# The first feed-forward stage grouped 4, 6, 6, 6 like the second, and low weight parts made by accumulating DMAs

## The chip, the cores and the metric

The kernel runs on one core of a Trainium2 chip. The metric is the device time in microseconds (us) of one execution; three runs of the kernel before took 881.19, 881.35 and 881.50 us, a median of 881.35. TensorE (PE) multiplies, VectorE (DVE), ScalarE (ACT) and GpSimd (POOL) work elementwise, SyncE (SP) issues most of the DMAs, and POOL can issue DMAs as well.

## The reference

One layer of an encoder on 512 positions of width 1024, in float32; the two feed-forward halves are what the change touches:

```python
def swiglu(h, w_gate, w_up, w_down):
    return (jax.nn.silu(h @ w_gate) * (h @ w_up)) @ w_down      # D_FF = 2752

x = x + 0.5 * swiglu(rms_norm(x, ffn1_norm), ffn1_w_gate, ffn1_w_up, ffn1_w_down)
h = rms_norm(x, mix_norm); u = h @ w_in          # Fourier mixer, attention
...
x = x + concat([f_out, a_out]) @ w_out
x = x + 0.5 * swiglu(rms_norm(x, ffn2_norm), ffn2_w_gate, ffn2_w_up, ffn2_w_down)
return rms_norm(x, final_norm)
```

## The kernel before

Every float32 operand is split in two parts: the high part is the value rounded to TensorE's fp32r format, the low part is the rest. A product of two such operands is three matmuls (`product`, L100 to L103): high by high, high by low, low by high. For a weight tile the high part is a cast on ACT (L96) and the low part a subtraction on VectorE (`lows`, L72): `lo = raw - hi`. The raw tile comes by a DMA on SP's queue (`raw_tile`, L85 to L88) into one of three buffers.

The hidden width of 2752 is cut into 21 columns of 128 and a tail "t" of 64. A feed-forward stage (`ffn`) goes through its columns in four groups; after each group the down products of its columns are added to `x`, one for each of the eight blocks `d` of the output (`down`, with weights `raw_dn`; `residual`, L390).

A column is computed in one of two ways. In the first group it is *plain*: a gate and an up product (`gate(c)`, c = 2j and 2j + 1), each of 8 x 3 = 24 matmuls with 512 columns; `evacuate` multiplies by the norm's row, applies the silu and splits the result into `at`. In later groups it is made of *seven products* of half the size (`seven`, L304): 7 x 4 x 3 = 84 matmuls with 256 columns, whose weight operands are sums of quarters (`prepare`), and whose moving operands `rt` are made once for a stage, in four steps, by `operands`, between the plain gates. Group g's seven-products are run ahead by one column: the first group holds its last plain column over to the second group (`rest`).

The weights' parts lie in slots of 4 KB for each partition: the ring has 12, of which 8 hold the normalised input (`hh`, `hl`) in the first group and become the pool of the seven-products later; the other 4 rotate (`plain`, `slot()`). In a first group four more are lent from free places of `at` (`lent`): two are handed back (`back(lent[:2])`) after the opening, two before the last gate.

The stage's opening makes the first gates: in stage 1 four together (`opening1`: columns 0 and 1), in stage 2 two, one behind the other (column 0). The tail's gate follows (`gate(2 * NF)`), then the other plain gates (`left`). In the last group of a stage the first two down products start without the group's last column, and that column's ending (`rest`) stands between them.

The orders on PE and SP are as written (`in_order`); those on ACT, VectorE and POOL are made by the framework's scheduler. The power of each norm, which the norm's row needs, runs on POOL (L160), and so do three loads ahead of the mixing stage (L842).

Of the kernel before, what the change touches and what calls it, by code (L numbers as in the profile page):

```python
# [9 lines left out]
AF = mybir.ActivationFunctionType  # L10
ALU = mybir.AluOpType
# [5 lines left out]
KD = D // P  # L17
F = 2752
NF = F // P
# [5 lines left out]
FILL_LEAD = 0.1  # L25
NS = 12

GROUPS1 = ((0, "t", 1, 2, 3), range(4, 10), range(10, 15), range(15, 21))
GROUPS2 = ((0, "t", 1, 2), range(3, 9), range(9, 15), range(15, 21))
PLACES = 7  # L30
HALF = S // 2
USES = "a11", "a12", "s1", "s2", "s4", "s3", "a22"
# [6 lines left out]
def asf(ap):  # L39
    return ap.bitcast(F32)  # L40
# [3 lines left out]
def encoder(ctx, tc, A, out):  # L44
    nc = tc.nc
# [36 lines left out]
    def weight_slots():  # L82
        return (slot().rearrange("p (a b) -> p a b", b=P) for _ in range(2))

    def raw_tile(src, name, n=KD):  # L85
        raw = wp.tile([P, KD, P], F32, tag="raw", name=f"raw_{name}")
        nc.sync.dma_start(out=raw[:, :n, :], in_=src)
        return raw  # L88

    def weights(src, name, n=KD, raw=None):  # L90
        raw = raw or raw_tile(src, name, n)
        hi, lo = weight_slots()
        if name in HI_DVE:
            nc.vector.tensor_copy(hi[:, :n, :], raw[:, :n, :])
        else:
            nc.scalar.copy(hi[:, :n, :], raw[:, :n, :])  # L96
        lows(lo[:, :n, :], raw[:, :n, :], hi[:, :n, :])
        return hi, lo
# [76 lines left out]
            nc.scalar.copy(self.rb[:, t], ps[:, t])  # L175
            return ps

    def ffn(norm, after, wgu, wd, wdt, groups, opening, closing):

        n_ = norm.n
        n_plain = len(groups[0])
        with tc.tile_pool(name=f"act{n_}", bufs=1) as ap, tc.tile_pool(name=f"sums{n_}", bufs=2) as sp:
            at = ap.tile([P, PLACES, 2, S], F32R, name=f"at{n_}")
            rt = ap.tile([P, 7, 2, KH, HALF], F32R, name=f"rt{n_}")
# [6 lines left out]

            own, shared = slots[:KD], slots[KD:]

            def gate(c, between={}):
                whi, wlo = weights(wgu[c], f"gu{n_}_{c}")
                ps = bank(f"gu{n_}_{c}")
                for k in range(KD):  # L200
                    between.get(k, int)()
                    product(ps, whi[:, k, :], wlo[:, k, :], hh[k], hl[k], k == 0, k == KD - 1)
                return ps
# [34 lines left out]
            def back(ts):  # L238
                plain[:] = [t for t in plain if all(t is not q for q in ts)]
# [12 lines left out]
            def prepare(j, most=False):  # L252

                g = sp.tile([P, KD * P], F32, tag="raw_g", name=f"raw_g{n_}_{j}")
                u = wp.tile([P, KD * P], F32, tag="raw", name=f"raw_u{n_}_{j}")
                for t, c in ((g, 2 * j), (u, 2 * j + 1)):
                    nc.sync.dma_start(out=t.rearrange("p (a b) -> p a b", b=P), in_=wgu[c])
                a11, a12, a21, a22 = g[:, :S], g[:, S:], u[:, :S], u[:, S:]
                s12 = sp.tile([P, 2 * S], F32, tag="s12", bufs=1, name=f"s12_{n_}_{j}")
                s34 = sp.tile([P, 2 * S], F32, tag="s34", bufs=1, name=f"s34_{n_}_{j}")  # L260
                w = {}

                def both(names, src):
                    hi, lo = (take(most and names[0] != "a11") for _ in range(2))
                    nc.scalar.copy(hi, src)  # L265
                    lows(lo, src, hi)
                    for i, n in enumerate(names):
                        w[n] = tuple(t[:, i * S : (i + 1) * S] for t in (hi, lo))
                    w[max(names, key=USES.index), "slots"] = hi, lo

                def single(n, src):
                    t = take(False)
                    hi, lo = t[:, :S], t[:, S:]
                    nc.scalar.copy(hi, src)
                    lows(lo, src, hi)
                    w[n] = hi, lo
                    w[n, "slots"] = (t,)

                def combine(out, a, b, op):
                    nc.vector.tensor_tensor(out=out, in0=a, in1=b, op=op)  # L280

                return w, [
                    (both, ("a11", "a12"), g),
                    (combine, s12[:, :S], a21, a22, ALU.add),
                    (combine, s12[:, S:], s12[:, :S], a11, ALU.subtract),
                    (both, ("s1", "s2"), s12),
                    (single, "a22", a22),
                    (combine, s34[:, :S], a11, a21, ALU.subtract),
                    (combine, s34[:, S:], a12, s12[:, S:], ALU.subtract),
                    (both, ("s3", "s4"), s34),  # L290
                ]
# [100 lines left out]
                )  # L392

            every = slice(0, S)
            for gi, group in enumerate(groups):
                last = gi == len(groups) - 1
                ahead = []
                if gi:
                    rest = seven(range(group[0] + 1, min(group[-1] + 2, NF)), ready)
                else:  # L400
                    lent = [at[:, i].rearrange("p a b -> p (a b)") for i in range(PLACES - 4, PLACES)]
                    plain.extend(lent)
                    row = []
                    pss = dict(enumerate(opening(gate, lambda: norm.column([norm.acc]), lambda: row.append(norm.row()))))
                    back(lent[:2])
                    due, parts, left = [*pss, "t"], list(range(KH)), range(2 * len(pss), 2 * n_plain)
                    pss["t"] = [gate(2 * NF)]
                    tail_weights()
                    for i, c in enumerate(left):
                        if c == left[-1]:  # L410
                            back(lent)
                        pss.setdefault(c // 2, []).append(gate(c))
                        if due:
                            j = due.pop(0)
                            evacuate(at[:, place(j)], n_, pss[j], norm)
                        if c % 2 and c != left[-1]:
                            due.append(c // 2)
                        while len(parts) * len(left) > (len(left) - 1 - i) * KH:
                            o = parts.pop(0)
                            operands(row[0], o, o + 1)  # L420

                    def rest():
                        evacuate(at[:, place(n_plain - 1)], n_, pss[n_plain - 1], norm)

                def added(d, ps):
                    residual(d, ps, every)
                    if last:
                        (after.sums if closing else after.add)(d)
                    if ahead:
                        f, *a = ahead.pop(0)  # L430
                        f(*a)

                waiting = []
                for d in range(KD):
                    if last and d == KD - 2:
                        back(lent)
                        if closing:
                            closing([(e, down(e, group, gi)) for e in (d, d + 1)], residual)
                            break
                    ps = bank(f"dn{n_}_{d}_{gi}")  # L440
                    steps = down(d, group, gi)(ps, every)
                    for _ in range(len(group) - (last and d < 2)):
                        next(steps)
                    waiting.append((d, ps, steps))
                    if d == 1 and not last:
                        ready = prepare(groups[gi + 1][0] + 1)
                        ahead.extend(ready[1])
                    if d == 0:
                        rest()
                        if last:  # L450

                            lent = slots[KD - 2 : KD]
                            plain[:0] = lent
                            continue
                    for d_, ps, steps in waiting:
                        for _ in steps:
                            pass
                        added(d_, ps)
                    waiting = []
                for f, *a in ahead:  # L460
                    f(*a)
                free.extend(where[j] for j in group)

    def evacuate(at, n_, pss, norm):
# [32 lines left out]
    n0, n1 = Norm(0), Norm(1)  # L497
# [42 lines left out]
        return [pss[0:2], pss[2:4]]  # L540

    with in_order():
        ffn(n0, n1, A["wgu1"], A["wd1"], A["wdt1"], GROUPS1, opening1, None)


    n2 = Norm(2)
    with tc.tile_pool(name="mix", bufs=1) as mp, tc.tile_pool(name="mixt", bufs=1) as mt:
# [281 lines left out]
        scale = HD**-0.5  # L829
# [95 lines left out]
    n3 = Norm(3)  # L925

    ready = (3, 4, 5)
# [50 lines left out]
        finish(2, 4)  # L978

    with in_order():  # L980
        ffn(n2, n3, A["wgu2"], A["wd2"], A["wdt2"], GROUPS2, lambda gate, column, row: [[gate(0, {KD - 1: column}), gate(1, {3: row})]], closing)


def _order():
# [101 lines left out]
```

## Time and profile before

| | |
|---|---|
| runs | 881.19, 881.35, 881.50 us |
| the profiled execution | 882.0 us, span 880.1 us, mean granted PE clock 0.995 |
| busy of the span | PE 863.1 us, VectorE 640.4, ACT 451.0, POOL 24.7 |
| stage 1, from the page's rows and the timeline | opening to 31.4 us, the tail's gate and six plain gates to 70.1, first group's down products to 96.0, seven-products and down products to 353.2 |
| mixing stage | 353 to about 524 us |
| stage 2 | about 524 us to the end |
| DMA | 83.37 MB on SP's queue, 1.32 MB on POOL's |

A PE matmul of 512 columns has a duration of 395 ns in the rows, but the next one starts about 0.23 us later; one of 256 columns has 283 ns and a step of 0.12. So the steps between starts are used for sums, not the durations. "idle <-" names what ended an engine's wait.

### The profile page before, as it was taken

How to read it: one execution, taken by the hardware profiler on the slowest of the kernel's cores; microseconds unless marked ns; L12 is line 12 of the kernel's file. 1: busy time of each engine (PE TensorE's matmuls, PEld its weight loads, DVE VectorE, ACT ScalarE, POOL GpSimd, SP SyncE). 2: the span in 40 equal slices, each digit the busy share in tenths (PEclk: the TensorE clock that was granted, in tenths of full speed). 3: DMA queues.
4: the chain of work that ended last, by engine and by line, in shares of the span. 5: the costliest groups of instructions: out<-in, count | busy, mean ns of one | idle time of the engine just before them, and what ended most of it. 6: DMA issues, size and time to landing. Idle time of an engine off the chain costs nothing.

```text
span 880.1 us, 13432 instructions
## 1 busy us (share of the span) xinstructions
PE 863.1 (98%) x5334; PEld 766.7 (87%) x5334; DVE 640.4 (73%) x1003; ACT 451.0 (51%) x746; POOL 24.7 (3%) x32
## 2 busy tenths in 40 slices
PE   8999999999999999999999999999999999999995
PEld 5888999889989988888888888889998999889985
DVE  7798788459757837699888558977975688469444
ACT  7454466226525634677775436535652365327432
POOL 0000000000000000211000000000000000000002
PEclk9999999999999999999999999999999999999998
DMA  7324232333243113521110223242224232322212
GB/s 245 112 67 164 98 118 86 99 116 104 69 141 114 55 36 108 204 83 37 50 48 25 94 67 127 75 141 97 108 79 140 88 119 69 105 110 85 73 36 96
DMA packets 29150, 85.55 MB, mean 97 GB/s; under 512 B 3488, under 2 KB 6560, under 8 KB 28960
## 3 DMA queue, kind: packets, MB, share of 16 engines
q1 hardware_dynamic: 28560, 83.37, 28.1%
q0 software_dynamic: 384, 1.32, 0.5%
q8 instruction: 41, 0.67, 0.3%
q14 instruction: 21, 0.17, 0.1%
q10 hardware_dynamic: 144, 0.02, 0.0%
HBM read 81.81 MB, written 2.10 MB: 95 GB/s over the span
## 4 chain that ended last, share of the span: by engine, by line
PE 56%; issue 39%; DVE 2%; ACT 2%; DMA 1%; POOL 0%; SPq 0%; POOLq 0%; ACTq 0%; DVEq 0%
PE r L304 10%; PE q L304 5%; PE dn L103 4%; PE dn L101 4%; PE dn L102 4%; PE p L304 3%; PE gu L103 2%; PE gu L102 2%; PE gu L101 2%; PE out L101 2%; PE out L103 2%; PE out L102 2%; PE pt L790 1%; PE q L101 1%; PE q L102 1%
## 5 line engine op out<-in xcount | busy, mean ns | idle before, releaser
L304 PE MATMUL r<-rt,ring 128*128 128x256 f32 x1584 | 207.2, 283 | 0.0
L304 PEld LDWEIGHTS r<-rt,ring 128*128 128x128 f32 x1584 | 196.1, 188 | 2.4
L101 PE MATMUL dn<-at,ring 128*128 128x512 f32 x324 | 128.0, 395 | 0.8 <-ACT ring L96 0.8
L103 PE MATMUL dn<-at,ring 128*128 128x512 f32 x324 | 127.9, 395 | 0.3 <-DVE ring L72 0.3
L102 PE MATMUL dn<-at,ring 128*128 128x512 f32 x324 | 127.9, 395 | 0.0
L390 DVE SCALAR_TENSOR_TENSOR xt<-dn,xt 128x512 f32<-128x512 f32 x62 | 42.8, 690 | 89.4 <-PE dn L103 89.4
L304 PE MATMUL q<-rt,ring 128*128 128x256 f32 x792 | 104.8, 282 | 0.0
L96 ACT CAST ring<-raw_dn 128x768 fp32r<-128x768 f32 (+3 forms) x64 | 48.1, 754 | 108.2 <-PE dn L102 89.8
L304 PEld LDWEIGHTS q<-rt,ring 128*128 128x128 f32 x792 | 98.7, 188 | 0.0
L72 DVE TENSOR_TENSOR ring<-s,ring 128x1024 fp32r<-128x1024 f32 x66 | 80.3, 1220 | 16.7 <-PE r L304 9.7
L265 ACT CAST ring<-s 128x1024 fp32r<-128x1024 f32 x66 | 69.3, 1050 | 37.4 <-PE r L304 19.2
L103 PEld LDWEIGHTS dn<-at,ring 128*128 128x128 f32 x324 | 61.0, 188 | 15.2 <-DVE ring L72 0.7
L101 PEld LDWEIGHTS dn<-at,ring 128*128 128x128 f32 x324 | 60.9, 188 | 14.8 <-ACT ring L96 1.0
L102 PEld LDWEIGHTS dn<-at,ring 128*128 128x128 f32 x324 | 60.9, 188 | 13.9
L72 DVE TENSOR_TENSOR ring<-raw_dn,ring 128x768 fp32r<-128x768 f32 (+3 forms) x64 | 54.5, 854 | 11.3 <-ACT ring L96 8.9
L304 PE MATMUL p<-rt,ring 128*128 128x256 f32 x396 | 52.4, 282 | 0.0
L72 DVE TENSOR_TENSOR ring<-raw_g,ring 128x1024 fp32r<-128x1024 f32 x33 | 40.4, 1223 | 15.5 <-PE p L304 10.9
L304 PEld LDWEIGHTS p<-rt,ring 128*128 128x128 f32 x396 | 49.3, 188 | 0.0
L265 ACT CAST ring<-raw_g 128x1024 fp32r<-128x1024 f32 x33 | 34.6, 1049 | 22.9 <-PE r L304 9.9
L101 PE MATMUL gu<-ring 128*128 128x512 f32 x112 | 44.1, 394 | 0.9 <-ACT ring L527 0.9
L102 PE MATMUL gu<-ring 128*128 128x512 f32 x112 | 43.9, 392 | 0.0
L103 PE MATMUL gu<-ring 128*128 128x512 f32 x104 | 41.1, 395 | 0.8 <-DVE ring L72 0.7
(308 smaller groups left out, 1514.0 us busy)
## 6 DMA issues: line engine op xcount, KB each, us to landing
raw_g<-in_wgu SPq DMA_DIRECT2D x33, 512.0 KB, 3.7
raw_u<-in_wgu SPq DMA_DIRECT2D x33, 512.0 KB, 4.3
raw_dn<-in_wd SPq DMA_DIRECT2D x40, 384.0 KB, 3.0
raw_gu<-in_wgu SPq DMA_DIRECT2D x16, 512.0 KB, 3.6
raw_o<-in_wo SPq DMA_DIRECT2D x8, 512.0 KB, 3.5
raw_in<-in_wins SPq DMA_DIRECT2D x6, 512.0 KB, 4.1
raw_dn<-in_wd SPq DMA_DIRECT2D x8, 320.0 KB, 2.9
raw_dn<-in_wd SPq DMA_DIRECT2D x8, 256.0 KB, 2.6
```

The source lines that it names most:

```text
L72: nc.vector.tensor_tensor(out=lo, in0=src, in1=asf(hi), op=ALU.subtract)
L96: nc.scalar.copy(hi[:, :n, :], raw[:, :n, :])
L101: nc.tensor.matmul(ps, whi, mhi, start=first, stop=False)
L102: nc.tensor.matmul(ps, whi, mlo, start=False, stop=False)
L103: nc.tensor.matmul(ps, wlo, mhi, start=False, stop=last)
L265: nc.scalar.copy(hi, src)
L304: nc.tensor.matmul(ps, a[:, ks], b[:, i], start=first and i == 0 and o == 0, stop=i == KH - 1 and o == 2, skip_group_check=not first,)
L390: nc.vector.scalar_tensor_tensor(out=x[d][:, t], in0=ps[:, t], scalar=0.5, in1=x[d][:, t], op0=ALU.mult, op1=ALU.add)
L790: nc.tensor.transpose(pt[:, c * P : (c + 1) * P], prob[t, b, c][:, kc * P : (kc + 1) * P], ident)
```

## The change

The first stage gets the second stage's groups: 4 plain columns less one held over, that is (0, t, 1, 2), then columns 3 to 8, 9 to 14 and 15 to 20; before it was (0, t, 1, 2, 3), 4 to 9, 10 to 14 and 15 to 20. So column 4 of the first stage is made by seven products, and `left` is four gates instead of six, with one `operands` step behind each.

In both stages the tail's gate and the gates in `left` get their low part in another way (`summed`): ACT casts the high part, ACT writes its negative into the low slot, and a DMA issued by POOL reads the weights from HBM again and adds them to the slot. That is five gates in stage 1 and seven in stage 2.

The two lent slots that were handed back before the last gate are kept until the first group's down products are done.

```diff
-GROUPS1 = ((0, "t", 1, 2, 3), range(4, 10), range(10, 15), range(15, 21))
-GROUPS2 = ((0, "t", 1, 2), range(3, 9), range(9, 15), range(15, 21))
+GROUPS = ((0, "t", 1, 2), range(3, 9), range(9, 15), range(15, 21))
...
+    def summed(src, name):
+        raw = raw_tile(src, name)
+        hi, lo = weight_slots()
+        nc.scalar.copy(hi, raw)
+        nc.scalar.activation(lo, asf(hi), AF.Copy, scale=-1.0)
+        nc.gpsimd.dma_start(out=lo, in_=src, accum_op=ALU.add)
+        return hi, lo
...
-            def gate(c, between={}):
-                whi, wlo = weights(wgu[c], f"gu{n_}_{c}")
+            def gate(c, between={}, make=weights):
+                whi, wlo = make(wgu[c], f"gu{n_}_{c}")
...
                     back(lent[:2])
                     due, parts, left = [*pss, "t"], list(range(KH)), range(2 * len(pss), 2 * n_plain)
-                    pss["t"] = [gate(2 * NF)]
+                    pss["t"] = [gate(2 * NF, make=summed)]
                     tail_weights()
                     for i, c in enumerate(left):
-                        if c == left[-1]:
-                            back(lent)
-                        pss.setdefault(c // 2, []).append(gate(c))
+                        pss.setdefault(c // 2, []).append(gate(c, make=summed))
...
                 for f, *a in ahead:
                     f(*a)
+                if not gi:
+                    back(lent)
```

The opening's weights, the down weights, the tail's down weights and the seven-products' weights still get their low part on VectorE.

More of the change, by code (lines that the diff above doesn't have):

```diff
@@ L176, in row, with ffn @@
             return ps
-    def ffn(norm, after, wgu, wd, wdt, groups, opening, closing):
+    def ffn(norm, after, wgu, wd, wdt, opening, closing):
         n_ = norm.n
-        n_plain = len(groups[0])
+        n_plain = len(GROUPS[0])
         with tc.tile_pool(name=f"act{n_}", bufs=1) as ap, tc.tile_pool(name=f"sums{n_}", bufs=2) as sp:
@@ L394, in ffn @@
             every = slice(0, S)
-            for gi, group in enumerate(groups):
-                last = gi == len(groups) - 1
+            for gi, group in enumerate(GROUPS):
+                last = gi == len(GROUPS) - 1
                 ahead = []
@@ L445, in ffn @@
                     if d == 1 and not last:
-                        ready = prepare(groups[gi + 1][0] + 1)
+                        ready = prepare(GROUPS[gi + 1][0] + 1)
                         ahead.extend(ready[1])
@@ L542, in encoder @@
     with in_order():
-        ffn(n0, n1, A["wgu1"], A["wd1"], A["wdt1"], GROUPS1, opening1, None)
+        ffn(n0, n1, A["wgu1"], A["wd1"], A["wdt1"], opening1, None)
     n2 = Norm(2)
@@ L980, in encoder @@
     with in_order():
-        ffn(n2, n3, A["wgu2"], A["wd2"], A["wdt2"], GROUPS2, lambda gate, column, row: [[gate(0, {KD - 1: column}), gate(1, {3: row})]], closing)
+        ffn(n2, n3, A["wgu2"], A["wd2"], A["wdt2"], lambda gate, column, row: [[gate(0, {KD - 1: column}), gate(1, {3: row})]], closing)
 def _order():
```

## The prediction

> **What bounds the kernel now.** The page comes first: busy shares, then the slices.
>
> ```profile
> PE 863.1 (98%) x5334; PEld 766.7 (87%) x5334; DVE 640.4 (73%) x1003; ACT 451.0 (51%) x746; POOL 24.7 (3%) x32
> ...
> PE   8999999999999999999999999999999999999995
> PEld 5888999889989988888888888889998999889985
> DVE  7798788459757837699888558977975688469444
> ```
>
> TensorE (PE) is busy from end to end, so time changes only if it gets less work or if a wait of it appears or goes. The windows over the two stages' first groups show what is near to becoming a wait:
>
> ```profile
> 40.00:60.00 20.00, 20.00 (x89) 16.30 (x88) 19.94 (x30) 10.97 (x14) 0.00 (x0) 1.00 0.25 80
> 60.00:80.00 20.00, 20.00 (x88) 16.31 (x87) 19.15 (x29) 10.30 (x16) 0.00 (x0) 1.00 0.34 109
> 540.00:560.00 20.00, 20.00 (x89) 16.32 (x88) 19.88 (x30) 11.32 (x14) 0.00 (x0) 1.00 0.25 86
> ```
>
> The columns are the window, its length, and busy time of PE, PEld, DVE, ACT and POOL. VectorE (DVE) is full, ScalarE (ACT) half idle, POOL empty, PE without a gap. The timeline around 320 us has the one wait of PE between the opening and the mixing stage, first on ACT, then on PE:
>
> ```profile
> 321.68 0.83 ACT L96 CAST ring<-raw_dn 128x768 fp32r<-128x768 f32 x1 [4.43 <-PE r L304]
> ...
> 320.18 1.58 PE L304 MATMUL r<-rt,ring 128*128 128x256 f32 x12
> 322.56 0.50 PE L101 MATMUL dn<-at,ring 128*128 128x512 f32 x1 [0.80 <-ACT ring L96]
> 322.90 0.40 PE L102 MATMUL dn<-at,ring 128*128 128x512 f32 x1
> 323.56 0.50 PE L103 MATMUL dn<-at,ring 128*128 128x512 f32 x1 [0.26 <-DVE ring L72]
> ```
>
> The cast of a down product's weights waited until PE had read the last seven-product out of the same slot. Last, the DMA view, for the price of a transfer on POOL's queue beside SP's:
>
> ```profile
> raw_gu<-in_wgu SPq DMA_DIRECT2D x16, 512.0 KB, 3.6
> ...
> raw_dn<-in_wd SPq DMA_DIRECT2D x8, 256.0 KB, 2.6
> ...
> pos<-in_pos POOLq DMA_DIRECT2D x1, 1028.0 KB, 7.6
> ...
> chan<-in_chan POOLq DMA_DIRECT2D x1, 256.0 KB, 4.3
> ```
>
> **Part 1, the groups.** Column 4 of the first stage moves from the plain form to the seven products. Plain it was 2 gates of 24 matmuls of 512 columns, which start 0.232 us apart (839.72 to 857.37 in 76 steps): 11.1 us. As sevens it is 84 matmuls of 256; one column of sevens follows another in 10.1 us (113.25 to 123.35). PE gains 1.0 us. The down products keep their number: 21 columns and the tail, four groups.
>
> The groups from 3 on now have the second stage's sizes, 6, 6 and 6, so the ring's slots rotate as there. In the built program's order on ACT all of the last group's first three weight casts stand ahead of the last column's seven-products, as in the second stage, whose passage at 816 to 830 us has no PE wait. So the wait at 321 us goes. The last seven-product's matmul starts at 320.18 + 11 x 0.119 = 321.49 and the next start is 1.07 us on instead of 0.12; the three steps after it are 0.34, 0.66 and 0.33 instead of 0.23. The excess is 0.95 + 0.11 + 0.43 + 0.10 = 1.6 us.
>
> The first group gets shorter, and its VectorE work with it, but not all of it. Two gates less are 11.1 us of PE, eight down products of 11 matmuls instead of 14 another 8 x 0.70 = 5.6 us; the four operand steps and the first group's evacuations that remain are squeezed into that. In the new order VectorE must do, after the last gate's end, nine instructions up to the low part of the third down product: the up half times the row (0.69), a low part of operands (1.22), gate times up (0.69), the low part of raw_g (1.22), a sum (0.69), a residual (0.69), a sum (0.69), the low part of raw_u (0.69), and the weights' low part for three columns (0.55). Each starts about 0.09 before the one ahead is over (rows 60.33 to 81.4 in VectorE's timeline), so the chain takes 0.17 + 5.86 + 0.55 = 6.6 us. PE needs the last after two down products of 11 and two more matmuls: 24 x 0.232 = 5.6 us. A new wait of 1.0 us, from 0 (if VectorE's up half starts ahead of its place) to 1.2. In the second stage the order differs and the low part stands early.
>
> **Part 2, the sums by DMA.** For twelve gates (tail and columns 2 and 3 in the first stage, tail and columns 1 to 3 in the second) it removes a VectorE subtraction of 1.22 us, 14.6 us in all, and adds an ACT negation of about 1.05 (the cast of the same tile; not shown with a scale, whose 128x512 row is 0.72 against 0.62) and 512 KB more from HBM on POOL's queue. The work on ACT lies beside PE: it is half idle there. VectorE's relief pays nothing by itself, since PE did not wait for it. What counts is the new latency of the low part: negation, POOL's issue, landing. The first sum of each stage stands ahead of the power of the norm on POOL; POOL issues it at about 23.6 us in the first stage (tail's cast, the wdt cast ending at 22.5, negation) and the power comes at 25.7, so with 0.6 for an issue (chan's row: 0.61) it is not late; the same in the second.
>
> Where does latency show? A low part can be prepared when its slot is free. Six slots rotate: tail takes two, wdt one, column 2's gate the fourth and the first lent one. That lent slot holds the high part of the opening's last weights, read until the opening's end at 31.4 us (the other lent slot's cast waits for PE until 31.58). So the negation starts one gate, the tail's, ahead of its use: 24 x 0.232 + 0.46 to the third matmul = 6.0 us, less 1.05 for the negation and 0.1 of handing on: **4.9 us** for the DMA. In the second stage the same holds for column 1's gate, whose slot the second gate frees at 535.9. The next gate has the same rhythm, but a late first one gives it that much more; the later ones have two gates of time. Behind the waiting negation on ACT stand the next gate's cast, the first operand casts and column 0's evacuation; PE uses none of them within the next 10 us. Behind a waiting sum on POOL stand only the later sums.
>
> How long does the DMA take? No row shows a sum. A copy of 256 KB took 4.3 us on POOL's queue; on SP's the step from 256 to 512 KB costs 3.6 - 2.6 = 1.0, so a copy of 512 KB by POOL is some 5.3. A sum also reads the 512 KB that it adds to: between nothing and another 2.0, so 5.3 to 7.4; pos, with 1028 KB, took 7.6, but was issued 0.6 behind chan's 256 KB and had about 1 us of that ahead of it. I take 6.5, what is left of pos: as many bytes as the sum moves in. That makes 6.5 - 4.9 = 1.6 us of wait in each stage, 3.2 together; ends: 0.4 each at 5.3 and 2.7 each at 7.6, below that nothing.
>
> [...]
>
> **Part 3, lent slots.** Two more slots for the first group's down weights: no added instruction. They let weights be cast one product earlier; the before's casts already kept up in the second stage (no PE gap at 575 to 597), so nothing.
>
> **Sum.** -1.0 - 1.6 + 1.0 + 3.2 = +1.6 us. The profiled execution took 882.0 us (span 880.1); the runs' median of 881.35 is 0.65 below that, and I carry the sum over to it: 881.35 + 1.6 = 883.0, at the edge of 0.2% (1.8 us), about what a measurement of this kernel can tell from no change.
>
> **The rivals.** [...]
>
> *The sums are slow*, beyond 7.6 us. Then the gates wait not once but in turn, since a slot comes free only with the gate that stands one or two ahead. At 8.5 each stage loses 3.6, and the second, with six gates of this kind, some 1 more: -1.6 + 7.2 + 1 = +6.6, 888 us. It decides from where the second of two sums waits as well, about 8 us. For it: each of the 128 rows needs two sources, and the source is read beside the raw loads on the same engines. Against: at a quarter of the DMA's capacity in use, queueing is small; one 1028 KB transfer stayed under 7.6. [...]
>
> *The regrouping does not remove the wait at 321 us*: +1.6 on top, 884.6. The order on ACT speaks against it.
>
> **Chances.** Sum between 5.3 and 7.6 us: 0.55, from about -0.8 to +3.8, of which 0.30 within the bound and 0.25 above. Quick: 0.20, of which 0.08 also without VectorE's wait and so below the bound. Slow: 0.20. The rest, 0.05, mostly the wait that stays. So faster 0.10, within 0.2% 0.42, slower 0.48. The range reaches from the quick case to the slow one at 8.5 us: 879.5 to 888.0.
>
> **What will show it.** The DMA view's rows from in_wgu on POOL's queue with their landing time (forecast 6.5); PE's waits at the third matmul of column 2's gate near 38 us and of column 1's in the second stage, each that time less 4.9; a wait of 1.0 on VectorE at the third down product near 66 us; none on ACT near 320; 84 more matmuls of 256. I am wrong if waits of PE stand at more gates than these two, or if the landing is under 5 us.

## The result, and the profile after

Five runs of the changed kernel took 884.80 to 886.91 us, median **885.79**; five of the kernel before in the same series 881.19 to 882.00, median 881.50. The ratio is 1.0047, 95% interval 1.0036 to 1.0058: **slower by 0.47%**. The forecast was 883.0 us, +1.6 in its own sum; the medians differ by +4.3, the two profiled executions by +3.0 (884.97 against 882.0; spans 883.2 and 880.1, +3.1). The three longer runs of the changed kernel also have a lower mean granted clock (0.993 and 0.994 against 0.996); this is taken up below.

The page's busy line and slices, in the changed kernel:

```profile
PE 862.2 (98%) x5370; PEld 767.1 (87%) x5370; DVE 632.5 (72%) x998; ACT 464.6 (53%) x765; POOL 35.2 (4%) x44
...
PE   8999999999999999999999999999999999999995
PEld 5788999899989998888888887889998999889985
DVE  7788986489746847699888558677975688469443
```

PE works 0.9 us less and the span is 3.1 us longer: all of the loss is waiting. PE has 36 matmuls more (two plain gates of 24 gone, 84 seven-product matmuls come). The windows over the first groups show where it waits; the first line is the one window of the kernel before that was not shown yet, the other four are the changed kernel's:

```profile
20.00:40.00 20.00, 20.00 (x94) 16.48 (x93) 14.64 (x25) 9.29 (x12) 1.05 (x1) 1.00 0.33 108
...
20.00:40.00 20.00, 18.33 (x86) 14.78 (x85) 13.53 (x26) 12.29 (x16) 3.76 (x4) 1.00 0.68 172
40.00:60.00 20.00, 20.00 (x88) 16.35 (x87) 18.16 (x30) 13.45 (x19) 1.72 (x2) 1.00 0.56 122
60.00:80.00 20.00, 19.06 (x82) 15.15 (x81) 17.23 (x26) 7.83 (x12) 0.00 (x0) 1.00 0.52 181
540.00:560.00 20.00, 17.87 (x76) 13.95 (x75) 17.39 (x30) 15.62 (x20) 3.43 (x4) 1.00 0.87 196
```

The figure behind the window's length is PE's busy time: now 1.67, 0.94 and 2.13 us short in three windows that were full before. VectorE's, two figures on, is down from 19.9 to 17.4 in the second stage, and that bought nothing there. The second-last column is the DMA engines' share: 0.25 before at 540 us, 0.87 now. The timeline of PE, with two rows of VectorE, gives the places (L109 to L111 are now the product's three matmuls, L95 the sum; L478 is the last gate's up half times the row, L71 a low part):

```profile
37.09 0.39 PE L110 MATMUL gu<-ring 128*128 128x512 f32 x1
39.15 0.50 PE L111 MATMUL gu<-ring,at 128*128 128x512 f32 x1 [1.67 <-DMA at<-in_wgu]
...
61.17 0.69 DVE L478 TENSOR_TENSOR u0p<-gu,rb 128x512 f32<-128x512 f32 x1 [1.94 <-PE gu L111]
...
67.05 0.55 DVE L71 TENSOR_TENSOR at<-raw_dn,ring 128x384 fp32r<-128x384 f32 x1
67.66 0.51 PE L111 MATMUL dn<-at 128*128 128x512 f32 x1 [0.94 <-DVE at L71]
...
322.46 1.60 PE L312 MATMUL r<-rt,ring 128*128 128x256 f32 x12
323.89 0.40 PE L109 MATMUL dn<-at,ring 128*128 128x512 f32 x1
...
543.20 0.50 PE L111 MATMUL gu<-ring 128*128 128x512 f32 x1 [0.45 <-DMA ring<-in_wgu]
...
550.62 0.50 PE L111 MATMUL gu<-ring,at 128*128 128x512 f32 x1 [1.68 <-DMA at<-in_wgu]
```

In excess over the normal step of 0.23, with the slower restart of some 0.1 us behind each wait (0.34 from 39.15 to the next start, at 39.49), the waits are 1.9 us at column 2's gate in the first stage, 1.2 at the third down product, 0.7 and 1.9 at column 1's two gates in the second. At 322 us nothing waits: 12 steps of 0.119 lie between the two rows. The DMA view and the sums' own line:

```profile
raw_gu<-in_wgu SPq DMA_DIRECT2D x14, 512.0 KB, 4.2
ring<-in_wgu POOLq DMA_DIRECT2D x7, 512.0 KB, 6.2
at<-in_wgu POOLq DMA_DIRECT2D x5, 512.0 KB, 6.3
...
L95 POOL DMA_DIRECT2D ring<-in_wgu x7: 857/861/923, 23.5 to 565.2; - x7
```

A sum lands 6.2 to 6.3 us after its issue in the median (5.2 to 8.0 over the twelve); issuing it takes POOL 0.86 us.

### The profile page after: what moved, and what is told of

Its sections match the earlier page's. It is cut to its first block, busy times and chain, and to the rows that moved or that the text cites. A ratio compares the mean times of both kernels' runs of the same rounds, so it can differ in the third digit from the quotient of the medians.

```text
span 883.2 us, 13557 instructions
## 1 busy us (share of the span) xinstructions
PE 862.2 (98%) x5370; PEld 767.1 (87%) x5370; DVE 632.5 (72%) x998; ACT 464.6 (53%) x765; POOL 35.2 (4%) x44
## 4 chain that ended last, share of the span: by engine, by line
PE 90%; DVE 3%; issue 2%; DMA 2%; ACT 2%; POOL 1%; SPq 0%; POOLq 0%; ACTq 0%; DVEq 0%
PE r L312 22%; PE q L312 11%; PE dn L111 8%; PE dn L109 8%; PE dn L110 8%; PE p L312 5%; PE gu L111 3%; PE gu L110 3%; PE gu L109 3%; PE out L109 2%; PE out L111 2%; PE out L110 2%; DMA at<-in_wgu 2%; PE pt L798 1%; PE q L109 1%
## 5 line engine op out<-in xcount | busy, mean ns | idle before, releaser
L312 PE MATMUL r<-rt,ring 128*128 128x256 f32 x1632 | 213.2, 283 | 0.0
L312 PEld LDWEIGHTS r<-rt,ring 128*128 128x128 f32 x1632 | 201.9, 188 | 2.4
L110 PE MATMUL dn<-at,ring 128*128 128x512 f32 x309 | 122.0, 395 | 0.0
L109 PE MATMUL dn<-at,ring 128*128 128x512 f32 x309 | 122.0, 395 | 0.0
L111 PE MATMUL dn<-at,ring 128*128 128x512 f32 x309 | 121.9, 395 | 0.0
L312 PE MATMUL q<-rt,ring 128*128 128x256 f32 x816 | 107.9, 281 | 0.0
L312 PEld LDWEIGHTS q<-rt,ring 128*128 128x128 f32 x816 | 101.6, 188 | 0.0
L104 ACT CAST ring<-raw_dn 128x768 fp32r<-128x768 f32 (+1 forms) x59 | 45.5, 775 | 100.5 <-PE dn L110 79.1
L71 DVE TENSOR_TENSOR ring<-s,ring 128x1024 fp32r<-128x1024 f32 x68 | 82.8, 1220 | 17.8 <-PE r L312 10.7
L111 PEld LDWEIGHTS dn<-at,ring 128*128 128x128 f32 x309 | 58.1, 188 | 13.9
L109 PEld LDWEIGHTS dn<-at,ring 128*128 128x128 f32 x309 | 58.1, 188 | 13.3
L110 PEld LDWEIGHTS dn<-at,ring 128*128 128x128 f32 x309 | 58.1, 188 | 13.3
L71 DVE TENSOR_TENSOR ring<-raw_g,ring 128x1024 fp32r<-128x1024 f32 x34 | 41.6, 1223 | 17.5 <-PE p L312 11.3
L71 DVE TENSOR_TENSOR ring<-raw_dn,ring 128x768 fp32r<-128x768 f32 (+1 forms) x54 | 49.0, 911 | 4.4 <-PE r L312 2.7
L282 ACT CAST ring<-raw_u 128x512 fp32r<-128x512 f32 x34 | 21.1, 621 | 35.5 <-PE dn L110 14.1
L109 PE MATMUL gu<-ring 128*128 128x512 f32 x96 | 37.8, 394 | 1.4 <-ACT ring L535 1.4
L110 PE MATMUL gu<-ring 128*128 128x512 f32 x96 | 37.6, 392 | 0.0
```

What stands on the lines that cost most here:

```text
L71: nc.vector.tensor_tensor(out=lo, in0=src, in1=asf(hi), op=ALU.subtract)
L109: nc.tensor.matmul(ps, whi, mhi, start=first, stop=False)
L110: nc.tensor.matmul(ps, whi, mlo, start=False, stop=False)
L111: nc.tensor.matmul(ps, wlo, mhi, start=False, stop=last)
L312: nc.tensor.matmul(ps, a[:, ks], b[:, i], start=first and i == 0 and o == 0, stop=i == KH - 1 and o == 2, skip_group_check=not first,)
```

## The experiments

Unless another kernel is named, every comparison is with the kernel before in the same series (medians 881.7 to 882.1). The waits quoted are PE's excess over its normal step, without the restart: in the changed kernel 1.8 us at column 2's gate, 1.1 at the third down product, 0.6 and 1.8 at column 1's gates.

**The sum's latency.** The addition is left out of the DMA, which becomes a plain copy from HBM; the low part is then the raw weight, so the subtraction is missing from the result.

```diff
-        nc.gpsimd.dma_start(out=lo, in_=src, accum_op=ALU.add)
+        nc.gpsimd.dma_start(out=lo, in_=src)
```

> The changed kernel with the same DMAs on POOL's queue as plain copies instead of sums (the subtraction of the high part is left out, so the low part is the raw weight); every wait and every byte from HBM is the same, only the read of the tile that is added to is gone. Packets of 4 KB take 0.327 us in the sums and 0.159 in SP's copies. Theory A (the second source is the price, eight packets for each of 16 DMA engines): landing 1.3 us earlier, 5.0 at the median instead of 6.3, waits of 0.6 to 1.3 us fewer at each of the three gates, total about 882.5 us. Rival (POOL's issue is the price, not the addition): landing stays above 6 us and the time at 885 to 886.

Measured 880.30 us, ratio 0.9982 (0.9973 to 0.9991).

```profile
ring<-in_wgu POOLq DMA_DIRECT2D x7, 512.0 KB, 3.8
```

No gate waits any more; the 1.1 us at the third down product stay. So the gates' waits, all of them, come from the 2.4 us by which a sum lands later than a copy of the same bytes by the same queue. The copies landed sooner than theory A had it (3.8 against 5.0), and the time fell further (880.3 against 882.5). In the traces a 4 KB packet of a sum holds its DMA engine for 0.327 us in the median, one of these copies for 0.174, one of SP's for 0.159; the packets of POOL's queue take 4.6% of the 16 engines' span with the sums and 2.9% with the copies. POOL takes 0.86 us to issue a sum and 0.53 for a copy.

**The groups alone.** The change without the sums:

```diff
-                    pss["t"] = [gate(2 * NF, make=summed)]
+                    pss["t"] = [gate(2 * NF)]
...
-                        pss.setdefault(c // 2, []).append(gate(c, make=summed))
+                        pss.setdefault(c // 2, []).append(gate(c))
```

> The groups 4, 6, 6, 6 and the kept lent slots, but all low parts by VectorE's subtraction as before. Theory A (the loss is the sums' latency at the gates whose low slot is free only one gate ahead): the waits at the gates' third matmul (1.9 us in the first stage, 2.7 in the second in the changed kernel's trace) are gone. But VectorE gets five subtractions of 1.22 us back into a shorter first group, so the wait at the third down product (1.2 us) grows to some 3 to 4. Against before: -1.0 (sevens) -1.6 (wait at 321 us) +3.8 = +1.2, about 882.7 us. Theory B (the sums are what costs, VectorE's chain is covered): -1.0 -1.6 +1.2 = -1.4, about 880.1 us.

Measured 886.53, ratio 1.0048 (1.0035 to 1.006): as slow as the changed kernel, for another reason, and slower than either theory had it. No gate waits. At the first group's down products of the first stage PE waits 2.6 us on a cast of the down weights and another 1.4 on a low part, and from 66.5 us on the granted clock is at half for 6.83 us.

```profile
64.64 1.04 ACT L273 CAST ring<-raw_g 128x1024 fp32r<-128x1024 f32 x1 [1.29 <-PE dn L111]
65.96 0.62 ACT L282 CAST ring<-raw_u 128x512 fp32r<-128x512 f32 x1 [0.27 <-DMA raw_u<-in_wgu]
66.48 0.51 ACT L104 CAST ring<-raw_dn 128x384 fp32r<-128x384 f32 x1
```

The cast that PE needs (66.48) stands on ACT behind two casts for the first seven-product column, the first of which waits for PE itself. So without the sums the new groups do wait, where the prediction had put the sums' relief at nothing; whether the load on VectorE does it or the order on the queues is taken up below.

**The sums alone**, in the old groups and with the lent slots handed back as before (the two edits of the change that concern `summed`, put into the kernel before):

> The sums by DMA at the same gates, but the groups of before, so seven gates of the first stage and seven of the second have sums. Theory A: the waits at the gates stay (1.9 and 2.7 us, in the first stage as well), the wait at 321 us stays as in before, no wait at the third down product of the first group, since the first group has two gates more for VectorE: +4.6, about 886 us. If the regrouping itself (and not the sums) made the loss: within 1 us of before, 881 to 882.5.

Measured 890.15, ratio 1.009 (1.0076 to 1.0104). The wait at the first gate behind the tail's is 3.0 us, followed by 3.41 us at half clock; the second stage waits 0.8, 1.9 and 1.0; the old wait near 321 us stands (at 326 here). Theory A had 886: without the new groups the sums cost more than it said, and they have nothing to do with the wait at 321 us.

**A slot more in time.** One lent slot stays in use longer, so that a sum could start a gate earlier:

```diff
-                    back(lent[:2])
+                    back(lent[:1])
...
+                        if c == left[-1]:
+                            back(lent[:2])
```

> The changed kernel with one more lent slot kept through the gates (one is handed back after the opening instead of two, the second before the last gate), so that seven slots rotate and every low slot is free two gates ahead of its use: 6.0 + 5.6 - 1.1 = 10 us for the sum. Theory A: no wait at any gate, whatever the landing times; the wait at the third down product stays 1.2: -1.0 -1.6 +1.2 = -1.4 against before, about 880.1 us. Rival (the sums cost by their traffic, that is by slower raw loads and busier DMA engines): waits stay at the gates or move to casts that wait for raw tiles, 884 to 886 us.

Measured 891.97, ratio 1.0104 (1.009 to 1.0118): the wrong way, and slower than either theory had it. In the first stage the gate's wait did fall, to 0.6 us. In the second stage up to three sums are now in flight at once, all but the last land in 7.2 to 8.3 us (the median of all twelve is 7.5), and a gate waits 2.8. In the first stage the down products wait 2.2 us on a cast and 1.8 on a low part. That is not the sums: the last three there landed in 5.3 to 5.5, and the cast stands on ACT behind one for the first seven-product column that waits 1.9 us for its load. In both stages half clock follows (mean granted clock 0.989 in the profiled execution; 0.996 in the changed kernel's). More room made the sums of the second stage collide; what brought on the waits of the first was not tested on its own.

**The lent slots as before** (part 3 of the change undone):

```diff
+                        if c == left[-1]:
+                            back(lent)
                         pss.setdefault(c // 2, []).append(gate(c, make=summed))
...
-                if not gi:
-                    back(lent)
```

> The changed kernel with the two lent slots handed back ahead of the last gate, as in the kernel before; groups and sums stay. Theory A (the lent slots kept are worth nothing, as the prediction had it): the changed kernel's time within 1 us, the same waits of PE at the gates and 1.1 us at the third down product. Rival: the casts and sums of the first down products' weights come one slot later without them, and the wait behind the last gate grows by 1 to 2 us, with half clock behind it if it passes 2.5 us.

Measured 889.45, ratio 1.0084 (1.0071 to 1.0098), 3.7 us above the changed kernel's median. The last gates' sums now wait for a slot too: 1.1 us at 55 us and 1.0 at 577 on a DMA, and 0.9 at a late down product on VectorE. The two slots are worth what the prediction's "nothing" left out: they keep the sums from being late once more. The wait behind the last gate, where the rival looked, stayed at 1.2 us. Not all of the 3.7 us is theirs: behind the second stage's wait of 1.95 us, which in the changed kernel is 0.1 shorter, this trace has 3.41 us of half clock, and the changed kernel's has none.

**One gate less by sums** in the first stage, two in the second, those that had waited:

```diff
-                        pss.setdefault(c // 2, []).append(gate(c, make=summed))
+                        make = weights if c in ((4,), (2, 3))[n_ > 0] else summed
+                        pss.setdefault(c // 2, []).append(gate(c, make=make))
```

> The changed kernel, but the gates that waited (the first plain gate behind the tail's in the first stage, both of column 1 in the second) get their low part by VectorE's subtraction again; the other nine keep the sums. Theory A (a sum is late only where its slot comes free one gate ahead): no wait of PE at any gate, landings about 6 us; VectorE has 1.22 us more in the first stage, so the wait at the third down product is 1.1 to 2.3 us instead of 1.1, and no stretch of half clock follows. Against the kernel before: -1.0 - 1.6 + 1.1 to 2.3, so 0.3 to 1.5 us faster. Rival (the sums are late because they overlap, as they were with a seventh slot): a later gate waits instead, 1 to 2 us a stage, and the time stays about 3 us above the kernel before.

Measured 888.39, ratio 1.0072 (1.0058 to 1.0086). That is slower than either theory had it. The second stage is cured (the way from the norm's row, inside the last gate ahead of the tail's, to the first down product takes 43.0 us; 42.5 before, 45.4 changed). In the first the wait moved on by one gate (1.6 us at 43), as the rival had it, and at the third down product it grew from 1.1 to 3.6 us, with 6.83 us of half clock: far more than the one subtraction of 1.22.

**Down weights by sums.** On top of that, the low parts for the second and third down product of that group by sums (192 KB each):

> As the kernel with three gates less by sums, and the low parts of the second and third down product's weights of the first stage's first group come by sums too (384 KB each), which takes 2 x 0.55 us off VectorE's chain behind the last gate. Theory A: the wait at the third down product falls to between 0 and 1.2 us; against the kernel before -1.0 - 1.6 + 0 to 1.2: 1.4 to 2.6 us faster, and faster than both kernels. Rival: the sums of the down weights land after the products need them (their slots come free late), and PE waits 1 to 3 us on a DMA at the second or third down product: about the kernel before or slower.

Measured 886.97, ratio 1.005 (1.0038 to 1.0063). The wait at the third product is 3.5 us, now on the DMA. The sum itself took only 3.6 us to land; it was issued at 66.28, since the cast of these weights stands on ACT behind the last evacuation and behind the casts for the first seven-product column. What is late is the place in the queue, not the transfer: the rival's wait came, but not from late slots.

**Order instead of load.** The changed kernel, with one digit changed: the first group prepares the first seven-product column behind the third down product, not the second.

```diff
-                    if d == 1 and not last:
+                    if d == (1 if gi else 2) and not last:
```

> The changed kernel with one edit: in the first group of a stage the preparation of the first seven-product column (a cast, sums and low parts, 3.3 us of VectorE ahead of the third down product's low part) starts behind the third down product instead of the second. In the built order VectorE then makes that low part ahead of the up half that waits for the last gate. Theory A (the wait at the third down product comes from the order on VectorE's queue, not from how much work it has): that wait of 1.1 us goes, the gates' waits stay: 1.2 us less than the changed kernel, some 2.7 above the kernel before. Rival (VectorE is full, and what is put off comes late at the first seven-products near 86 us): a wait there of 1 to 3 us, and no gain.

Measured 884.05, ratio 1.0026 (1.0016 to 1.0037), 1.7 us less than the changed kernel's median. VectorE's timeline:

```profile
57.76 0.56 DVE L71 TENSOR_TENSOR at<-raw_dn,ring 128x384 fp32r<-128x384 f32 x1 [1.41 <-ACT ring L104]
...
60.90 0.68 DVE L478 TENSOR_TENSOR u0p<-gu,rb 128x512 f32<-128x512 f32 x1
```

The low part of the third down product's weights starts at 57.76 instead of 67.05: ahead of the up half that waits for the last gate (60.90), in a stretch in which the changed kernel's VectorE stood idle for 2.4 us (1.94 of them right ahead of 61.17). The group's down products take 20.5 us instead of 21.6, and the wait is gone. The gates' waits stay. This is as theory A had it.

**No sums, later preparation** (the groups alone, with the edit above):

> No sums at all: the groups and the lent slots of the changed kernel, all low parts by VectorE, with the later preparation. Theory A (order, not load): the waits of 2.6 us at the third down product and 1.4 behind it that the groups alone had go, and the half clock behind them with them; 0 to 0.6 us remain: against the kernel before 2.0 to 2.6 us faster. Rival (VectorE is too full without the sums: five subtractions of 1.22 us more ahead of 70 us): waits of 2 us or more stay at the down products, with half clock behind them, and the time is 1 to 5 us above the kernel before.

Measured 881.94, ratio 1.0001 (0.9992 to 1.0009): 4.6 us less than the groups alone, from one digit. Waits of 0.9 and 1.8 us are left at the first and fourth down product, none with half clock. So order was the larger part. Whether VectorE's load is the rest is not shown: the 0.9 us is a late evacuation of the tail, but the low part that the fourth product waits for again stands right behind four pieces of the preparation on VectorE (66.48 to 69.51), so the 1.8 us can be the digit once more.

**Two gates less by sums, later preparation** (first stage: the tail's and the last two gates keep sums; second: column 1 by subtraction):

> As the kernel with the later preparation, and in the first stage both gates behind the tail's, in the second both of column 1, get their low part by VectorE's subtraction; tail and the last gates keep the sums. Theory A (a sum waits only where its slot comes free one gate ahead and VectorE's order sets the other wait): no wait of PE over 0.5 us at any gate or down product; against the kernel before -1.0 - 1.6 + 0 to 0.5: 2.1 to 2.6 us faster, faster than both kernels. Rival (the sums' landings, 7 us where they overlap, hit the next gate each time): a wait of 1 to 2 us at the third gate behind the tail's, as the kernel with one gate less had at the second: 0 to 1 us faster than the kernel before.

Measured 882.91, ratio 1.001 (1.0001 to 1.0018). No gate waits, as theory A had it. But the fourth and the last down product wait 1.2 and 1.0 us on VectorE: the low part of their weights now stands behind the preparation's pieces, the last one behind a sum that itself waits 2.1 us for a load. The digit was not large enough. Together with the 2.6 us gained these waits would give 0.4 us less than the kernel before; the median is 1.0 above it, and the trace shows no single wait for the difference.

**All of it**: sums only for the tail's and the last two gates of the first stage, none in the second, and the first stage's preparation behind the fifth down product.

```diff
-                    pss["t"] = [gate(2 * NF, make=summed)]
+                    pss["t"] = [gate(2 * NF, make=summed if n_ in [0] else weights)]
...
-                        pss.setdefault(c // 2, []).append(gate(c, make=summed))
+                        make = summed if c in (() if n_ else (6, 7)) else weights
+                        pss.setdefault(c // 2, []).append(gate(c, make=make))
...
-                    if d == 1 and not last:
+                    if d == (1 if gi else 1 if n_ else 4) and not last:
```

> The groups of the change; sums only for the tail's gate and the last two plain gates of the first stage, whose slots come free with time to spare, VectorE's subtraction for the other two and for the whole second stage; and in the first stage the preparation of the first seven-product column starts behind the fifth down product, so that the low parts of the down products' weights stand ahead of it in VectorE's order. Theory A (each wait that is left comes from a sum with one gate of lead or from the order on VectorE's queue, and both are avoided here): no wait of PE over 0.3 us in the first stage from the opening to the seven-products; the way from the start of the gates to the first seven-products is 30.9 + 20.5 us instead of 32.8 + 21.6; against the kernel before -1.0 - 1.6: 2.2 to 2.7 us faster, faster than both kernels. Rival (VectorE is full there, 21 us of work in the 20.5 us of the down products): a wait of 1 us or more turns up at a later down product or at the first seven-products near 80 us, and the time is within 1.5 us of the kernel before.

Measured **878.96 us** (878.93 to 879.92), ratio 0.9971 (0.996 to 0.9982): 2.75 us faster than the kernel before, about as theory A had it, and 6.8 below the changed one's median. The windows:

```profile
20.00:40.00 20.00, 20.00 (x95) 16.48 (x94) 13.53 (x24) 10.98 (x14) 2.38 (x3) 1.00 0.54 144
40.00:60.00 20.00, 20.00 (x88) 16.34 (x87) 19.88 (x35) 12.87 (x18) 1.39 (x2) 1.00 0.47 96
60.00:80.00 20.00, 20.00 (x89) 16.22 (x88) 18.96 (x29) 8.72 (x13) 0.00 (x0) 1.00 0.54 184
```

PE is full in all three. VectorE is back at 19.88 of 20 us at 40 to 60 and that does no harm, since what PE needs next stands first in its queue. Three sums of 512 KB instead of twelve are left. What this does not tell apart: with the digit at 4 no run without sums was made, so the three sums' own share is open.

**The clock.** Half clock had turned up behind several of these waits. The kernel before, with eight deliberate ones:

```diff
...
+    def pause(ps, widths):
+        nc.scalar.activation(hold, ps[:, 0:8], AF.Copy, scale=0.0, bias=1.0)
+        for n in widths:
+            nc.gpsimd.tensor_tensor(out=hold[:, :n], in0=hold[:, :n], in1=mhalf[:, :n], op=ALU.pow)
+        nc.tensor.matmul(bank("hold")[0:8, 0:8], hold, hold, start=True, stop=True)
...
+                        if (n_, gi, d_) in WAITS:
+                            pause(ps, WAITS[n_, gi, d_])
```

> The kernel before with eight deliberate waits of PE, each behind a down product in a steady stretch (second and third group of each stage, third and seventh product): a chain of small powers on POOL that starts from the product's result and ends in an 8x8 matmul. By POOL's rows (1.05 us for 4 columns, 1.64 for 8, 0.53 for 1, 0.70 for 2) plus about 0.8 of handing on, the waits are about 1.9, 3.6, 2.5, 4.1, 3.0, 3.6, 3.0 and 3.2 us, 25 in sum; nothing else is changed, and the output is the same. Theory A (a wait from about 2.5 us on is followed by 3.41 or 6.83 us at half clock): six or seven stretches of half clock, each worth 1.7 to 3.4 us, and the time 35 to 49 us above the kernel before. Rival 1 (half clock only behind waits over 3.4 us): three stretches, 30 to 35 above. Rival 2 (the half clock of the earlier runs had another cause): none, 25 above.

Measured 924.73, 42.9 above the kernel before. The waits came out at 2.7 to 4.0 us, 27.9 in sum, and behind every one of them the clock is at half for 3.41 (six times) or 6.83 us (twice). The remaining 15.0 us are what that cost: 34.1 us at half clock, in which PE did not always have work. Two of the waits and what follows, in windows (the third-last column is the granted clock):

```profile
189.90:192.10 2.20, 0.30 (x2) 0.00 (x0) 1.29 (x2) 0.18 (x1) 1.55 (x1) 1.00 0.00 0
192.20:198.90 6.70, 5.26 (x14) 4.21 (x15) 0.00 (x0) 0.00 (x0) 1.30 (x2) 0.50 0.00 0
793.10:796.20 3.10, 0.30 (x2) 0.00 (x0) 1.56 (x2) 0.91 (x2) 2.01 (x1) 1.00 0.16 36
796.40:803.00 6.60, 5.80 (x15) 4.56 (x16) 0.00 (x0) 1.05 (x1) 0.67 (x2) 0.50 0.34 129
```

Theory A's condition held, though no wait under 2.5 us came about, so that this run does not show where the limit lies; rival 1, with a limit of 3.4 us, falls, since waits of 2.7 and 3.1 us had it too. The 2.5 us of theory A was the author's estimate: 2.6 us (the groups alone), 2.8 (a slot more) and 3.0 (the sums alone) had half clock behind them, 1.8 in the changed kernel had none; the kernel with the lent slots as before has it behind 1.95. The total lies in the middle of theory A's 35 to 49.

## Why the prediction came out as it did

**Right.** The regrouping: column 4 as sevens and the wait at 321 us. The last version, which has no other wait left, is 2.75 us faster by medians and 2.9 by spans (877.2 against 880.1); the two terms forecast 2.6. The third down product: 1.0 forecast, 1.2 measured, by the chain of nine instructions that was written down (61.17 to 67.60 in VectorE's timeline). The first stage's gate: 1.6 forecast, 1.9 measured, at the matmul named, and on a landing of 6.3 us against 6.5; the rest is a lead of 4.6 us in place of 4.9, most of it because POOL issued the sum 0.3 us behind the negation and not 0.1. That the landing came out so close is luck in its parts: it was built on a copy of 5.3 us and at most 2.0 for the addition, and the plain copy took 3.8, so that the addition costs 2.4. Single sums landed in 5.2 to 8.0 us, single copies by the same queue in 3.7 to 5.6.

**Mis-sized: the second stage's gates.** Forecast was one wait of 1.6, behind which "a late first one gives it that much more". Measured were two, 0.7 and 1.9, and 2.9 us more from the norm's row to the first down product. With the first stage's gate three gates waited, which by the prediction's own sign (waits at more gates than two) makes it wrong here. The step that failed is one landing time for all sums. The first landed in 5.2 us, its gate hardly waited, and so gave the next one nothing; that one's sum was in flight beside raw loads and the next sum and took 7.1. The DMA engines' share of 0.87 in that window is what "a quarter of the DMA's capacity in use" had left out: the sums' own packets. By the profiled executions the sum then closes: -1.0 - 1.6 + 1.2 + 1.9 + 2.9 = +3.4, against +3.1 of the spans.

**Wrong, though it hid itself: VectorE's relief "pays nothing by itself", and the lent slots "nothing".** Both were judged against the old groups, in which PE did not wait for VectorE. The new ones wait some 4 us at the down products, with half clock, when they have no sums (the groups alone), of which the sums leave 1.1; and without the two slots the time is 3.7 us longer. Since the later preparation alone takes away the half clock and leaves 2.7 us of these waits, it is open how much of the sums' credit is relief and how much another order on ACT and VectorE. The change as a whole came out within its range because these two credits stand against costs that only appear without them, which is luck. The rival in which the regrouping leaves the 321 us wait is refuted; the slow case (beyond 7.6 us) did not come in the median, but single landings of 7.7 to 8.0 show it was near.

**Missing: the clock.** The medians differ by 1.3 us more than the profiled executions. The changed kernel's trace shows no half clock until the kernel's end (from 875 us). The kernel with the lent slots as before has nearly the same wait at the same gate of the second stage, 0.1 us longer, and behind it this (windows of its trace, before and after the clock's change):

```profile
551.10:554.40 3.30, 1.50 (x7) 1.18 (x7) 3.30 (x6) 3.23 (x5) 0.04 (x1) 1.00 0.97 196
554.60:557.90 3.30, 3.30 (x10) 2.53 (x9) 2.43 (x5) 0.68 (x2) 0.86 (x1) 0.50 0.81 145
```

The wait is 2.0 us here, and the granted clock goes from 1.00 to 0.50 behind it. A stretch of this kind in the changed kernel's three longer runs would explain the 1 to 2 us that they take more and their lower clock: 3.41 us at half clock lower the mean of 885 us by 0.002, and the two executions on trace with one such stretch have 0.993. Those three runs left no trace, so this is argued, not shown.

## What to carry to other kernels

A wait that goes in one place says nothing of the order behind it: before work is moved to another engine or queue because one engine is full, look at what stands in front of the late instruction on that engine, and whether it idles just ahead of it; one digit was worth more here than twelve transfers. A transfer that replaces an instruction brings its latency (6.3 us here for a subtraction of 1.22) into every place where the buffer comes free late; use it only where the buffer comes free with more time than that to spare, as for the three sums of the last version, on which no gate waits, and expect its landing to vary (5.2 to 8.0 us here). Price each part of a change against the other parts, not against the kernel before alone: relief that is worth nothing there can be what makes the rest bearable.

## What the runs showed of the hardware

**The granted clock.** Over all these traces the changes of the clock lie on one grid of 3.413 us within each run: differences of their times are multiples of it (870.40 us, 255 steps, between the two changes in the changed kernel's trace; 866.99 us, 254 steps, in that of the kernel before). PE's idle time was added up in each step of that grid, from the starts of its matmuls: ahead of the half clock in which every trace ends, all fifteen stretches of half clock begin behind a step with 2.0 to 3.3 us of idle time, and no step at full clock with less than 2.0 has one behind it (those of 2.0 to 2.1 go either way). In the changed kernel the largest idle time of a step ahead of the last has 1.9 us (547.7 to 551.1 us) and no half clock behind it. So a wait of 1.8 us was cheap here. One just over 2 can cost up to 1.7 us more by an estimate from these numbers (half of 3.41), or twice that where half clock lasts for two steps; in the kernel with deliberate waits ten steps of half clock cost 15.0 us, 1.5 each. What makes it last was not worked out.

**Sums by DMA.** A sum of 512 KB lands in 5.2 to 8.0 us in the changed kernel where a copy by the same queue takes 3.8 in the median, and its 4 KB packets hold an engine about twice as long (0.327 us against 0.174 for that copy's and 0.159 for SP's). The overlap of sums is not all of it: the changed kernel's slowest, 8.0 us (issued at 23.55), had no other sum in flight but about 1.2 MB of SP's loads beside it; the one issued at 47.37 had neither and took 5.3. Nor do the loads' bytes alone account for it: the sum issued at 528.61 took 5.4 us beside 0.7 MB of them, the one at 565.20 took 7.3 beside 0.3. With a seventh slot, where sums overlap more, the median was 7.5 us.
